# The start of a decoder layer: the first two weight chunks in two halves each, their transfers on two queues, three more warm-up matmuls

## The chip, the cores and the metric

One core of one Trainium2 chip runs the whole kernel. The metric is the time of one execution on the device in microseconds (us). Kernels are compared by the median of several executions; the profile is of one further execution, taken with the hardware profiler.

## The reference

The kernel computes one layer of a hybrid decoder for a sequence of 256 tokens with 1024 features, all in float32, and a last RMS norm:

```
h = rms_norm(x, norm_mix)
z = h @ w_in                      # 1024 -> 3072 columns
a_x, a_y, b_q, b_f, b_i, b_g, c_q, c_k, c_v = split(z)
y = concat(norm(rglru(a_x, a_y)), hgrn2(b_q, b_f, b_i, b_g), norm(attention(c_q, c_k, c_v)))
x = x + y @ w_out
x = x + square(relu(rms_norm(x) @ w_ff1)) @ w_ff2
return rms_norm(x)
```

For this case only the beginning matters: the input projection h @ w_in, and what of the HGRN2 group follows first. That group takes b_f through a sigmoid (forget gate and key) and b_q through a silu (query), and multiplies the two.

## The kernel before, in words

**Precision by splitting.** Each float32 matrix is split into a high part that TensorE (PE) takes in one pass and a low part, the remainder. A product is then three matmuls: high by high, high by low, low by high (`mm3`, L275 to L279). The high part is a copy on ScalarE (ACT, L59), the low part a subtraction on VectorE (DVE, L60), which waits for the copy. For weights this is `split_w`, for the transposed input `x_split` (L130): the gain of the norm goes in there, while the norm's factor 1/rms, one per token, is applied to the results later.

**Tiles.** x stands transposed in xa, 128 features by 256 tokens in each of eight tiles k = 0 to 7, with a few small parameters in front. w_in comes as 12 chunks of 256 columns; a chunk is 128 x 2048 (1 MB), that is its eight k blocks side by side. A quarter of a chunk (256 KB) holds two k blocks and goes with one piece of x (two tiles). A chunk takes 48 matmuls of 256 columns: eight k blocks, two halves, three products each; that is 12 in each of its four slots. Three buffers hold raw chunks; `split_w` issues the load of chunk i + 3 when it has split the last part of chunk i.

**Order.** The order of work is written out by hand. `slots` (L765) is the list of PE's work, in units such as `in_quarter(i, q)`, a quarter of the matmuls of chunk i. `plan` (L769) says which other steps are put ahead of each slot. Each engine works through its own instructions in that order and waits, by semaphores, for what it needs from the others. In `in_quarter` (L291) chunk 0 goes over k outside and both halves of its columns inside, with two accumulators in the PSUM pool `mis`. All other chunks run one half of the columns over all eight k and then the other half, in one bank of the pool `acc`, which has four.

**Transfers.** All are issued by SyncE (SP). At the front it issues, in turn, the four pieces of x and the four quarters of chunk 0 (L100 to L104), then chunk 1 in four quarters, chunk 2 in two halves, and two small tensors (L107, L108). While this goes on, PE runs 9 matmuls on the identity into `warm` (L115), which nobody reads.

**Steps that the text names.** `small_lb` (L247): a few tiny operations on ACT, then on GpSimd (POOL), then on DVE (`omlb`, `lbm`). `x_sq` and `x_sum` (L190, L193): squares of x on ACT, and their sum over the eight tiles on DVE, three additions. `x_ss` (L198): sums over the features on PE (`xss`). `x_rms` (L204): 1/rms on DVE (`xv`) and POOL (`rx`). `x_bc` and `x_rb` (L210, L216): PE spreads rx over all partitions (`xbc`), ACT copies it to `RB`. `hg_f_ev` and `hg_q_ev` (L321, L334): DVE multiplies the results of chunks 0 and 1 by RB. `hg_f_act`, `hg_q_act`, `hg_q_dve` (L325 to L341): sigmoids and silu on ACT, each with a table load, and their product `qk` on DVE. `hg_dqk` (L348): PE matmuls on qk. Chunk 0 is b_f, chunk 1 b_q, chunk 2 b_g.

Of the kernel before, what the change touches and what calls it, by code (L numbers as in the profile page):

```python
# [8 lines left out]
F32 = mybir.dt.float32  # L9
# [3 lines left out]
OP = mybir.AluOpType  # L13
AX = mybir.AxisListType

P = 128
# [16 lines left out]
def trunk_kernel(ctx: ExitStack, tc, x, x_t, w_in, w_out, w_ff1, w_ff2, small, hg_norm, norm_final, out):  # L33
    nc = tc.nc
    V, A, G, T = nc.vector, nc.scalar, nc.gpsimd, nc.tensor
# [3 lines left out]
    raw_p = ctx.enter_context(tc.tile_pool(name="raw", bufs=RAW))  # L39
# [6 lines left out]
    def acc(name):  # L46
        return acc_p.tile([P, 512], F32, name=name, tag="acc")

    def mis(name):
        return mis_p.tile([P, 512], F32, name=name, tag="mis")  # L50

    def wt(name, shape, tag=None, bufs=None, dt=F32):
        return work.tile(shape, dt, name=name, tag=tag or name, bufs=bufs)
# [11 lines left out]
    NI = len(in_order)  # L65
    IG, IX, IY = 2, 3, 4
    NF = 16
    chunks = [w_in[c] for c, _ in in_order] + [w_out[j] for j in range(4)]
# [6 lines left out]
    raw, hi_w, lo_w = {}, {}, {}  # L75

    def load(i, n=1):
        if i < NCH:
            raw[i] = raw_p.tile([P, 2048], F32, name=f"raw{i}", tag="raw")
            for h in range(n):  # L80
                s_ = slice(h * 2048 // n, (h + 1) * 2048 // n)
                nc.sync.dma_start(raw[i][:, s_], chunks[i][:, s_])
# [13 lines left out]
    xT = xa[:, SP_WA:].rearrange("p (k t) -> p k t", k=KT)  # L96
    spw = const.tile([P, SP_N - SP_WA], F32, name="spw")
    hgn = const.tile([P, 64], F32, name="hgn")
    raw[0] = raw_p.tile([P, 2048], F32, name="raw0", tag="raw")
    for h in range(4):  # L100
        s_ = slice(h * 512, (h + 1) * 512)
        x_ = slice(SP_WA + h * 512 if h else 0, SP_WA + (h + 1) * 512)
        nc.sync.dma_start(xa[:, x_], x_t[:, x_])
        nc.sync.dma_start(raw[0][:, s_], chunks[0][:, s_])  # L104
    load(1, 4)
    load(2, 2)
    nc.sync.dma_start(spw, small)  # L107
    nc.sync.dma_start(hgn, bass.AP(tensor=hg_norm.tensor, offset=hg_norm.offset, ap=[[0, P], [1, 64]]))  # L108
# [3 lines left out]
    ident = const.tile([P, P], F32, name="ident")  # L112
    make_identity(nc, ident)
    warm = mis("warm")
    for n in range(9):  # L115
        T.matmul(warm[:, 0:128], ident, ident, start=True, stop=True)

    def rms_scale(ss, n, k, name):
# [38 lines left out]
    for L in LEVELS:  # L157
        n = 64 // L
# [27 lines left out]
    RB = wt("RB", [P, 256])  # L186
# [32 lines left out]
    def zT(i, dst):  # L219
        V.tensor_tensor(dst, z[i][2].rearrange("p (c t) -> p c t", c=2), RBb, op=OP.mult)  # L220
# [52 lines left out]
    z = {}  # L273
# [7 lines left out]
    def in_mm(i, half, k):  # L281
        o = z[i][half]
        s_ = slice(half * 128, (half + 1) * 128)
        wh = hi_w[i].rearrange("p (k c) -> p k c", c=CW)[:, k, :]
        wl = lo_w[i].rearrange("p (k c) -> p k c", c=CW)[:, k, :]
        if in_order[i][1] == CH:
            mm3(o, (wh[:, s_], wl[:, s_]), (hTh[:, k, :], hTl[:, k, :]), k == 0, k == KT - 1)
        else:
            mm3(o, (hTh[:, k, s_], hTl[:, k, s_]), (wh, wl), k == 0, k == KT - 1)

    def in_quarter(i, q):  # L291
        if q == 0:
            if i == 0:
                z[i] = [mis(f"z0{b}")[:, 0:256] for b in range(2)]
            else:
                a = acc(f"z{i}")
                z[i] = [a[:, 0:256], a[:, 256:512], a]
        if i == 0:
            for k in (2 * q, 2 * q + 1):
                for half in range(2):  # L300
                    in_mm(i, half, k)
        else:
            for k in range(4 * (q % 2), 4 * (q % 2) + 4):
                in_mm(i, q // 2, k)
# [8 lines left out]
    qc = wt("qc", [P, 2, 256])  # L313
# [18 lines left out]
            V.tensor_scalar(kB[:, c, :], kB[:, c, :], omlb[:, c:c + 1], None, op0=OP.mult)  # L332

    def hg_q_ev():  # L334
        zT(1, qc)

    def hg_q_act():
        A.activation(flat(qc), flat(qc), AF.Silu)
# [417 lines left out]
    def x1_ss():  # L756
        for t in range(2):
# [4 lines left out]
    r2 = wt("r2", [P, 2])  # L762
    nfb = wt("nfb", [P, D], tag="oc")
    S_ = split_w
    slots = [(in_quarter, i, q) for i in range(NI) for q in range(4)]  # L765
    slots += [(wout_part, k, t, n) for k in range(4) for t, n in tn]
    slots += [(wout_part, k, t, n) for t, n in tn for k in range(4, 8)]
    slots += [(ff1_first, c, kg) for kg in range(2) for c in range(2)]
    plan = {  # L769
        0: [  # L770
            (S_, 0, 0, 4), (x_split, 0), (x_split, 3), (x_split, 1), (S_, 0, 1, 4), (x_split, 5), (x_split, 4),
            (x_split, 2), (x_split, 7), (x_split, 6),
        ],
        1: [(S_, 0, 2, 4)],
        2: [(S_, 0, 3, 4), (S_, 1, 0, 4)],
        3: [(small_lb,), (S_, 1, 1, 4)],
        4: [(S_, 1, 2, 4), (x_sq, 0)],
        5: [(S_, 1, 3, 4), (x_sq, 1)],
        6: [(x_sum,)],
        7: [(x_ss,), (x_rms,), (small_lam,), (S_, 2, 0), (S_, 2, 1)],  # L780
        9: [(x_bc,), (S_, 3, 0), (S_, 3, 1)],
        10: [(x_rb,)],
        11: [(S_, 4, 0)],
        12: [(hg_f_ev,), (hg_q_ev,), (S_, 4, 1), (hg_f_act,)],
        13: [(S_, 5, 0), (hg_q_act,), (hg_q_dve,)],
        14: [(hg_f_dve,)],
# [66 lines left out]
    i = FI + 2  # L853
# [114 lines left out]
```

## Time and profile before

| | |
|---|---|
| median of 3 runs | 323.9 us (323.85, 323.9, 326.06) |
| profiled execution | 325.72 us |
| its span | 324.0 us |
| PE busy | 313.3 us (97%) |
| VectorE busy | 200.5 us (62%) |
| ScalarE busy | 172.3 us (53%) |
| GpSimd busy | 30.1 us (9%) |
| bytes moved by DMA | 54.65 MB, 169 GB/s on average |

The span is the time from the first to the last thing that the profiler records; the rest of the execution's time lies around it. All times in the rows count from the start of the span. A busy share of PE says that instructions were in it, not at which clock they ran. Matmuls overlap, so the distance of their starts is the time that one costs, and their own duration is longer. In the rows, PEld is PE's loading of the stationary operand, and SPq the queue of SyncE, which issues transfers.

### The profile page before, as it was taken

The page shows a single profiled execution, that of the slowest core. Times are in us where ns is not written, and L with a number is a line of the kernel's source. Part 1 is how long each engine was busy: PE and PEld are TensorE (multiplying, and loading weights), DVE is VectorE, ACT ScalarE, POOL GpSimd, SP SyncE. Part 2 cuts the span into 40 slices and gives each one's busy share as a digit, 9 for nine tenths or more (in the row PEclk, how much of TensorE's full clock was granted, in tenths as well). Part 3 has the DMA queues.
Part 4 walks back from the last instruction along what each step waited for, and adds up shares of the span by engine and source line. Part 5 has one row for each costly group of instructions (what it writes and reads, how often), then busy time and mean ns, then how long its engine had stood idle before and what let it go on. Part 6 is the DMA issues. An engine that isn't in the chain of part 4 may idle for free.

```text
span 324.0 us, 5150 instructions
## 1 busy us (share of the span) xinstructions
PE 313.3 (97%) x2090; PEld 286.1 (88%) x2090; DVE 200.5 (62%) x288; ACT 172.3 (53%) x281; POOL 30.1 (9%) x76
## 2 busy tenths in 40 slices
PE   6999999999999999999999999999999999999990
PEld 5899999988899988998898899889889988988980
DVE  1778999997736385498637635743763574376334
ACT  3968796665665372398525633652563365256114
POOL 8428600000002000000000000000000000000002
PEclk9999999999999999999999999999999999999998
DMA  7967353342018327038763365346336524630003
GB/s 195 364 260 284 143 225 131 131 138 121 2 31 358 131 95 296 0 132 324 261 259 141 129 251 224 99 199 259 144 122 254 227 92 202 261 129 3 0 0 129
DMA packets 9960, 54.65 MB, mean 169 GB/s; under 512 B 1232, under 2 KB 1488, under 8 KB 4176
## 3 DMA queue, kind: packets, MB, share of 16 engines
q1 hardware_dynamic: 9936, 54.32, 44.9%
q8 instruction: 16, 0.26, 0.3%
q14 instruction: 8, 0.07, 0.1%
HBM read 53.27 MB, written 1.05 MB: 168 GB/s over the span
## 4 chain that ended last, share of the span: by engine, by line
PE 94%; DMA 2%; issue 1%; ACT 1%; SPq 1%; POOLq 0%; POOL 0%; DVE 0%
PE f L277 9%; PE f L278 9%; PE f L279 9%; PE fo L278 9%; PE fo L277 9%; PE fo L279 9%; PE z L277 7%; PE z L278 7%; PE z L279 7%; PE wo L277 2%; PE wo L278 2%; PE wo L279 2%; DMA xa<-in_x_t_dram 2%; PE lv L372 2%; PE s L593 1%; PE pt L613 1%
## 5 line engine op out<-in xcount | busy, mean ns | idle before, releaser
L60 DVE TENSOR_TENSOR wl<-raw,wh 128x1024 fp32r<-128x1024 f32 (+1 forms) x100 | 112.9, 1179 | 17.2 <-ACT wh L59 15.4
L59 ACT CAST wh<-raw 128x1024 fp32r<-128x1024 f32 (+1 forms) x100 | 95.1, 1009 | 5.2 <-DMA raw<-in_w_in_dram 5.2
L277 PE MATMUL f<-x1h,wh 128*128 128x256 f32 x256 | 72.4, 283 | 0.0
L278 PE MATMUL f<-x1l,wh 128*128 128x256 f32 x256 | 72.4, 283 | 0.0
L279 PE MATMUL f<-x1h,wl 128*128 128x256 f32 x256 | 72.3, 283 | 0.0
L721 ACT ACTIVATE fr<-f 128x512 f32<-128x512 f32 (+1 forms) x17 | 9.7, 572 | 86.9 <-PE f L279 86.9
L723 DVE TENSOR_TENSOR fu<-fr 128x512 f32<-128x512 f32 (+1 forms) x17 | 11.2, 660 | 69.2 <-ACT fr L721 69.2
L278 PE MATMUL fo<-wl,uh 128*128 128x512 f32 x128 | 51.1, 399 | 0.0
L277 PE MATMUL fo<-wh,uh 128*128 128x512 f32 x128 | 50.4, 394 | 0.0
L279 PE MATMUL fo<-wh,ul 128*128 128x512 f32 x128 | 50.2, 392 | 0.0
L277 PEld LDWEIGHTS f<-x1h,wh 128*128 128x128 f32 x256 | 49.0, 191 | 0.7
L278 PEld LDWEIGHTS f<-x1l,wh 128*128 128x128 f32 x256 | 48.9, 191 | 0.6
L279 PEld LDWEIGHTS f<-x1h,wl 128*128 128x128 f32 x256 | 49.0, 191 | 0.0
L277 PE MATMUL z<-hTh,wh 128*128 128x256 f32 x128 | 38.9, 304 | 1.6 <-ACT hTh L131 1.6
L278 PE MATMUL z<-hTl,wh 128*128 128x256 f32 x128 | 37.8, 295 | 0.1
L279 PE MATMUL z<-hTh,wl 128*128 128x256 f32 x128 | 37.2, 291 | 0.0
L279 PEld LDWEIGHTS fo<-wh,ul 128*128 128x128 f32 x128 | 24.0, 188 | 5.7
L277 PEld LDWEIGHTS fo<-wh,uh 128*128 128x128 f32 x128 | 24.1, 188 | 5.5
L278 PEld LDWEIGHTS fo<-wl,uh 128*128 128x128 f32 x128 | 24.0, 188 | 4.9
L277 PEld LDWEIGHTS z<-hTh,wh 128*128 128x128 f32 x128 | 25.6, 200 | 2.6 <-ACT hTh L131 2.2
L278 PEld LDWEIGHTS z<-hTl,wh 128*128 128x128 f32 x128 | 25.6, 200 | 0.8 <-DVE hTl L132 0.7
L279 PEld LDWEIGHTS z<-hTh,wl 128*128 128x128 f32 x128 | 25.6, 200 | 0.0
(204 smaller groups left out, 424.2 us busy)
## 6 DMA issues: line engine op xcount, KB each, us to landing
raw<-in_w_ff_dram SPq DMA_DIRECT2D x32, 1024.0 KB, 4.8
raw<-in_w_in_dram SPq DMA_DIRECT2D x9, 1024.0 KB, 4.8
raw<-in_w_out_dram SPq DMA_DIRECT2D x4, 1024.0 KB, 4.8
raw<-in_w_in_dram SPq DMA_DIRECT2D x8, 256.0 KB, 6.8
raw<-in_w_in_dram SPq DMA_DIRECT2D x2, 512.0 KB, 6.3
xa<-in_x_dram SPq DMA_DIRECT2D x2, 512.0 KB, 7.3
xa<-in_x_t_dram SPq DMA_DIRECT2D x3, 256.0 KB, 6.8
out_dram<-ot SPq DMA_DIRECT2D x3, 256.0 KB, 2.0
```

The lines of the kernel that those rows point to most:

```text
L59: A.copy(hi, src)
L60: V.tensor_tensor(lo, src, hi.bitcast(F32), op=OP.subtract)
L277: T.matmul(o, lh, rh, start=first, stop=False)
L278: T.matmul(o, lh, rl, start=False, stop=False)
L279: T.matmul(o, ll, rh, start=False, stop=last)
L372: T.matmul(ps[:, g * 128:(g + 1) * 128], kB[:, hp, hs], rhs, start=True, stop=True)
L593: T.matmul(ps[:, 128:384], q[rows, c, 128:256], k[rows, c, 0:256], start=True, stop=True)
L613: T.transpose(pt[:, j * 128:(j + 1) * 128], pr_t[h][:, j * 128:(j + 1) * 128], ident)
L721: A.activation(r[:, s_], src, AF.Relu)
L723: V.tensor_tensor(u[:, s_], r[:, s_], r[:, s_], op=OP.mult)
```

## The change

The first two chunks are worked on together: PE takes the first two quarters (k = 0 to 3) of chunk 0, then those of chunk 1, then the last two quarters of chunk 0 and of chunk 1. For this chunk 1 gets two accumulators of its own from the pool `acc`, as chunk 0 has two from `mis`, and `hg_q_ev` reads them in two instructions. The four quarters of chunk 0 are issued by ScalarE; SyncE issues the pieces of x and chunk 1 in the new order. 12 instead of 9 matmuls on the identity run at the start. The plan of slots 0 to 11 is written anew: the x tiles are split in their order, `small_lb` follows the second quarter of chunk 1, `x_sum` stands between the two splits of chunk 2, `x_ss` and `x_rms` move from slot 7 to slot 9, `x_bc` from slot 9 and `x_rb` from slot 10 to slot 11. From slot 12 on the plan is the same.

```diff
-    raw[0] = raw_p.tile([P, 2048], F32, name="raw0", tag="raw")
-    for h in range(4):
-        s_ = slice(h * 512, (h + 1) * 512)
+    for i in range(2):
+        raw[i] = raw_p.tile([P, 2048], F32, name=f"raw{i}", tag="raw")
+
+    def part(eng, i, a, b):
+        eng.dma_start(raw[i][:, a * 512:b * 512], chunks[i][:, a * 512:b * 512])
+
+    def x_part(h):
         x_ = slice(SP_WA + h * 512 if h else 0, SP_WA + (h + 1) * 512)
         nc.sync.dma_start(xa[:, x_], x_t[:, x_])
-        nc.sync.dma_start(raw[0][:, s_], chunks[0][:, s_])
-    load(1, 4)
+
+    x_part(0)
+    part(nc.scalar, 0, 0, 1)
+    x_part(1)
+    part(nc.scalar, 0, 1, 2)
+    part(nc.sync, 1, 0, 1)
+    part(nc.scalar, 0, 2, 3)
+    part(nc.sync, 1, 1, 2)
+    part(nc.scalar, 0, 3, 4)
+    x_part(2)
+    x_part(3)
+    part(nc.sync, 1, 2, 4)
     load(2, 2)
...
-    for n in range(9):
+    for n in range(12):
         T.matmul(warm[:, 0:128], ident, ident, start=True, stop=True)
...
+            elif i == 1:
+                z[i] = [acc(f"z1{b}")[:, 0:256] for b in range(2)]
             else:
                 a = acc(f"z{i}")
                 z[i] = [a[:, 0:256], a[:, 256:512], a]
-        if i == 0:
+        if i < 2:
             for k in (2 * q, 2 * q + 1):
                 for half in range(2):
                     in_mm(i, half, k)
...
     def hg_q_ev():
-        zT(1, qc)
+        for c in range(2):
+            V.tensor_tensor(qc[:, c, :], z[1][c], RB, op=OP.mult)
...
-    slots = [(in_quarter, i, q) for i in range(NI) for q in range(4)]
+    slots = [(in_quarter, i, 2 * h + q) for h in range(2) for i in range(2) for q in range(2)]
+    slots += [(in_quarter, i, q) for i in range(2, NI) for q in range(4)]
...
-        0: [
-            (S_, 0, 0, 4), (x_split, 0), (x_split, 3), (x_split, 1), (S_, 0, 1, 4), (x_split, 5), (x_split, 4),
-            (x_split, 2), (x_split, 7), (x_split, 6),
-        ],
-        1: [(S_, 0, 2, 4)],
-        2: [(S_, 0, 3, 4), (S_, 1, 0, 4)],
-        3: [(small_lb,), (S_, 1, 1, 4)],
-        4: [(S_, 1, 2, 4), (x_sq, 0)],
-        5: [(S_, 1, 3, 4), (x_sq, 1)],
-        6: [(x_sum,)],
-        7: [(x_ss,), (x_rms,), (small_lam,), (S_, 2, 0), (S_, 2, 1)],
-        9: [(x_bc,), (S_, 3, 0), (S_, 3, 1)],
-        10: [(x_rb,)],
-        11: [(S_, 4, 0)],
+        0: [(S_, 0, 0, 4), (x_split, 0), (x_split, 1)],
+        1: [(S_, 0, 1, 4), (x_split, 2), (x_split, 3)],
+        2: [(S_, 1, 0, 4)],
+        3: [(S_, 1, 1, 4), (small_lb,)],
+        4: [(S_, 0, 2, 4), (x_split, 4), (x_split, 5)],
+        5: [(S_, 0, 3, 4), (x_split, 6), (x_split, 7)],
+        6: [(S_, 1, 2, 4), (x_sq, 0)],
+        7: [(S_, 1, 3, 4), (x_sq, 1)],
+        8: [(S_, 2, 0), (x_sum,), (S_, 2, 1)],
+        9: [(x_ss,), (x_rms,), (small_lam,), (S_, 3, 0), (S_, 3, 1)],
+        11: [(x_bc,), (x_rb,), (S_, 4, 0)],
         12: [(hg_f_ev,), (hg_q_ev,), (S_, 4, 1), (hg_f_act,)],
         13: [(S_, 5, 0), (hg_q_act,), (hg_q_dve,)],
```

## Rows read from the trace of the kernel before

**Rows 1.** Page, part 1: engine, busy us, share of the span, instructions.

```profile
PE 313.3 (97%) x2090; PEld 286.1 (88%) x2090; DVE 200.5 (62%) x288; ACT 172.3 (53%) x281; POOL 30.1 (9%) x76
```

**Rows 2.** PE's waits, whole run: us in total, times, longest us.

```profile
PE z L277 <- ACT hTh L131: 1.6, 2, 1.1
```

**Rows 3.** Window of PE on tile z: stretch, us, PE busy (matmuls), clock, DMA, GB/s.

```profile
6.80:14.16 7.36, 6.77 (x26) 1.00 1.01 366
```

**Rows 4.** Timeline of PE: start us, us, what, xcount, [idle before <-releaser].

```profile
1.46 4.21 PE L116 MATMUL warm<-ident 128*128 128x128 f32 x18 [1.46 <-POOL ident masks.py:199]
...
6.82 0.58 PE L277 MATMUL z<-hTh,wh 128*128 128x256 f32 x1 [1.14 <-ACT hTh L131]
...
10.87 0.58 PE L277 MATMUL z<-hTh,wh 128*128 128x256 f32 x1 [0.44 <-ACT hTh L131]
...
21.27 0.56 PE L201 MATMUL xss<-ones,xsq 128*128 128x64 f32 x4
...
23.15 0.28 PE L277 MATMUL z<-wh,hTh 128*128 128x256 f32 x1
...
24.63 0.60 PE L213 MATMUL xbc<-ident,rx 128*128 128x128 f32 x4
...
35.15 0.33 PE L351 MATMUL dqk<-bones,qk 128*128 128x64 f32 x2
```

**Rows 5.** Chain that ended last: start us, us on the chain, what.

```profile
12.22 0.21 PE z L277
...
14.95 0.12 PE z L277
```

**Rows 6.** Timeline of SP's queue, front.

```profile
0.81 0.38 SPq L103 DMA_DIRECT2D xa<-in_x_t_dram  x1
1.24 0.42 SPq L104 DMA_DIRECT2D raw<-in_w_in_dram  x1
...
10.87 0.33 SPq L107 DMA_DIRECT2D spw<-in_small_dram  x1
11.55 0.33 SPq L108 DMA_DIRECT2D hgn<-in_hg_norm_dram  x1
```

**Rows 7.** Timeline of ACT.

```profile
5.74 0.62 ACT L59 CAST wh<-raw 128x512 fp32r<-128x512 f32 x1 [3.65 <-DMA raw<-in_w_in_dram]
...
8.84 0.62 ACT L59 CAST wh<-raw 128x512 fp32r<-128x512 f32 x1 [0.45 <-DMA raw<-in_w_in_dram]
...
13.24 0.20 ACT L236 ACTIVATE sm<-sm 128x2 f32<-128x2 f32 x1
...
14.79 1.05 ACT L191 ACTIVATE xsq<-xa 128x1024 f32<-128x1024 f32 x1
...
17.22 1.98 ACT L59 CAST wh<-raw 128x1024 fp32r<-128x1024 f32 x2
...
25.27 0.37 ACT L217 COPY RB<-xbc 128x256 f32<-128x256 f32 x1 [3.01 <-PE xbc L213]
```

**Rows 8.** Timeline of DVE.

```profile
10.10 2.20 DVE L132 SCALAR_TENSOR_TENSOR hTl<-xa,hTh 128x256 fp32r<-128x256 f32 x5
12.32 1.90 DVE L60 TENSOR_TENSOR wl<-raw,wh 128x512 fp32r<-128x512 f32 x3
15.37 0.17 DVE L253 TENSOR_SCALAR omlb<-lb 128x2 f32<-128x2 f32 x1 [1.15 <-POOL lb L245]
...
17.35 1.23 DVE L194 TENSOR_TENSOR xsq<-xsq 128x1024 f32<-128x1024 f32 x1
...
19.34 0.43 DVE L196 TENSOR_TENSOR xsq<-xsq 128x256 f32<-128x256 f32 x1
...
21.94 5.92 DVE L60 TENSOR_TENSOR wl<-raw,wh 128x1024 fp32r<-128x1024 f32 x5
...
33.06 0.70 DVE L341 TENSOR_TENSOR qk<-qc,kB 128x512 f32<-128x512 f32 x1 [0.72 <-ACT qc L338]
```

## The prediction

> **What bounds the kernel now.** I read the busy shares first: PE is busy 313.3 of 324.0 us [rows 1]. A busy matmul row need not mean full pace, so the next view is PE's waits over the whole run: after the warm-up there are only two, both of the input projection on hTh, 1.6 us in all [rows 2]. From 10.87 us to the tail PE never waits. So whatever changes the time has to act either on the stretch before that, or on the order of later work so strongly that PE begins to wait again.
>
> Then I looked at the pace. In the stretch from 6.82 to 14.16 us the matmuls start 0.21 us apart, later 0.12 us [rows 5]. 256 columns in 0.21 us is the 1.2 GHz level; 0.12 us belongs to the 2.4 GHz level. The granted clock column says 1.00 there all the same [rows 3], so the pace has to be read from the spacing. Before the rise PE had worked without a pause since 10.87 us; ahead of that it had stood 1.14 us before the first projection matmul and 0.44 us before the thirteenth [rows 4]. 26 matmuls lie in that stretch of 7.34 us [rows 3]; at 0.12 us they would take 3.1 us. **4.2 us is therefore the most that the front can give**, 1.3% of the run.
>
> **The change, part by part.** The sum is made against the profiled execution: 325.72 us, of which the span is 324.0 us. That is 1.8 us above the median of 323.9 us.
>
> *More warm-up.* 18 records take 4.21 us [rows 4], 0.234 us each; 24 take 5.6 us and end near 7.07 us instead of 5.67. The first real matmul came at 6.82, so the three extra ones cost at most 0.25 us there and close the pause of 1.14 us.
>
> *Issue from ScalarE.* ACT issues four transfers before its first table load. SP needs 0.42 us for one, with starts 0.43 to 0.47 us apart [rows 6], so ACT has about 2 us of extra work in a stretch in which it waits for the first weights until 5.74 us [rows 7]. I cost this at nothing; if the weights came before about 4 us, it would delay the first cast. SP has four fewer issues ahead of its second chunk and of the small tensors behind it.
>
> *Landing.* Eight pieces of 256 KB (in either version) must land before 48 matmuls can run. Before, SP's last issue of the front, at 11.55 us, marks the landing of the eighth, because SP holds a new transfer back until an older one has landed; at the end pieces come 0.68 us apart (10.87 and 11.55) [rows 6]. Ends for the change: one piece later (+0.7 us), since the two queues interleave; or, had all pieces after the first weights (5.74) come 0.68 us apart, 9.8 us, which is 1.7 us earlier. I take 0.5 us earlier, nearer to no gain, because issues at 0.47 us run far ahead of landings: issuing was not what held the pieces back. The Trainium skill says the same in "DMA: Bandwidth & Descriptors", Issuing engines are not separate DMA queues: a second issuing engine saves only sequencer time, the transfers share the same DMA engines. By that rule the shift is 0 and the result half a microsecond later than by my choice.
>
> *Order of the halves.* The second quarter of chunk 0 no longer waits for x tile 2 behind tiles 5 and 4: ACT casts w01 at 8.84 [rows 7] and the x tiles 2 and 3 follow, so its matmuls start near 10.0 instead of 10.87. At full pace three quarters of 12 x 0.12 = 1.44 us bring PE to about 14.7 us.
>
> *The wait on small_lb.* Here DVE stops. The step now stands ahead of the split of w02. In the old trace the chain from ACT's exp (13.24) to DVE's omlb took until 15.54, 2.30 us, and DVE stood 1.15 us for it [rows 7, 8]; only chunk 1 was behind it. Now w02, w03, four low x tiles and everything after are behind it. With landing as before: w11 at 11.55, its cast 0.62 at most [rows 7], exp at 12.1, DVE free at 14.4. PE needs the low parts of w02 and x tile 4 at 14.7 and gets them at 14.4 + 0.63 + 0.44 = 15.5. Four more quarters then end near 21.2 us. Before, they ended at 23.15 less 0.36 us of xss matmuls: 22.8. **Gain up to here 1.6 us**, and this hardly depends on the clock: at the slow pace PE would reach 14.7 later, but DVE would still be there at 15.5.
>
> *x_sum between the two splits of chunk 2.* From 14.4 DVE has four weight splits (0.63 each, 2.52), four low x tiles (2.20/5 each, 1.76), the first split of chunk 2 (5.92/5 = 1.18), x_sum (17.35 to 19.77, 2.42) and the second split (1.18): 9.06 us, to 23.5 [rows 8]. ACT delivers the cast of chunk 2 late (four casts, four x tiles, two squares of 1.05 and half of 1.98 after 12.7 [rows 7]), about 0.8 us of waiting, so 24.3. PE, at 22.6 with the first quarter of chunk 2, waits for xss and then for this split. That quarter ends near 25.6, the next at 27.0. **More than half of the gain is gone.**
>
> *x_bc two slots later.* xbc moves from slot 9, 24.63 us, to slot 11, about 27.0. RB hangs on it, and on RB a chain on ACT and DVE without a pause: RB copy at 25.27 after 3.01 us of waiting, two casts, table load, two sigmoids, a cast, table load, silu, and qk on DVE, done at 33.76 [rows 7, 8]. From xbc's start that is 9.13 us. PE wants qk for dqk in slot 16, which was 35.15 [rows 4]: the slack was 1.39 us. Two slots fewer between the two are 2 x 1.44 = 2.88 us, so **PE now waits about 1.5 us at dqk**, a wait that did not exist. dqk starts at 27.0 + 9.13 = 36.1, that is 1.0 us later than before with landing unchanged, 0.5 us with my landing. Behind it DVE's next items (kB, qbd) are just in time for slot 17, and from there PE is continuous again, so the half microsecond stays to the end.
>
> *PSUM.* z1 takes two accumulators; z4 then waits for the evacuation of z1 instead of using a free one. That falls in slots 12 and 16, more than 3 us apart; nothing. Two half evacuations in place of one cost a few tenths on DVE behind the table load.
>
> **Sum:** 325.72 + 0.5 = 326.2 in an execution like the profiled one. Now the median. The two short runs (323.85, 323.90) lie 1.8 us below it. Part of that could be an earlier rise of PE's clock in them: the 14 matmuls from 10.87 to 14.16 at 0.12 would save 1.3 us. This part would not carry over, since the changed front is held by DVE at either pace. Then the result is 326.2 - 0.5 = 325.7. If all 1.8 us carry over, 324.4. One trace cannot separate these; I take 324.7, nearer to the second because nothing shows the first.
>
> **The rivals.**
> - *The gain is kept.* If the pieces land a microsecond or more earlier, lb is out of the way before PE gets there, and if ACT makes up time before qk, 1.6 us and a little more reach the end: about 323.0. For: the early pieces land far apart (5.74, 8.84) against 0.68 later. Against: the slack of 1.39 us is a fixed length and two slots exceed it.
> - *The clock.* With the pause before 6.82 closed, the 26 slow matmuls run at 0.12: 26 x 0.09 = 2.3 us; carried through in full, 325.7 - 2.3 = 323.4 or, from the median, as low as 321.6. The Trainium skill, "TensorE: Matmul & The Clock Gate", Why this matters for your kernels, advises continuous work to reach and hold the upper level. The old trace agrees, with 3.3 us of unbroken work ahead of the rise. Against: at that pace PE waits for pieces and DVE instead.
> - *Slower than before.* The interleaving of the two queues delays the eighth piece. From one piece (0.7 us) on, the chain through lb, the second split of chunk 2, xbc and qk passes every tenth on: 1.0 + 0.7 = 1.7, or 327.4 in an execution like the profiled one.
> - *It does nothing.* Clock and landing as before: this is the forecast at +1.0, since the order alone makes it.
>
> **Chances.** Forecast 0.60, gain kept 0.18, clock 0.10, slower 0.12. The forecast's own range is 323.6 to 326.4. For 8 in 10 I reach down to 322.1 for most of the two faster cases and up to 326.7. A difference under 1% (320.7 to 327.1) can't be told from no change: inside it 0.88, faster 0.05, slower 0.07. The ceiling of 4.2 us leaves little for over 1% faster.
>
> **What would show it.** After: matmuls 0.12 us apart well before 14 us; PE waiting near 14.7 for a low part on DVE; DVE idle over 1 us ahead of omlb; PE waiting for wl of chunk 2 near 23 to 24 us; xbc near 27; a new wait of dqk on qk, 1 to 2 us, the largest one of PE. Wrong, if dqk does not wait, if the eighth piece lands before 10.5, or if PE stays at 0.21 us past 14 us.

## The result and the profile after

The changed kernel takes 326.17 us (median of 9 runs, 325.96 to 327.62); before took 323.9 us in the same set (9 runs, 323.65 to 326.15). The ratio is 1.0063, 95% interval 1.0034 to 1.0092: 2.0 us slower, 1.1 to 3.0; the medians differ by 2.3 us. That is 0.6%, inside the 1% in which the prediction had put 0.88 of its chances, and inside its range; its single number, 324.7, was 1.5 us too low. The profiled execution takes 326.17 us with a span of 324.5, against 325.72 and 324.0 before: 0.45 us more, where the sum had said 0.5.

One fact is needed to read these numbers. The times of one kernel fall into groups: before, 6 of 9 runs lie from 323.65 to 324.18 and 3 near 326; after, 6 lie from 325.96 to 326.18 and 3 near 327.6. The profile of before is of its upper group, that of after of its lower. Experiments 4, 5 and 9 are about what makes the groups.

First the busy time of the page, then PE's waits over the whole run (us in total, times, longest), both of the changed kernel.

```profile
PE 312.4 (96%) x2096; PEld 285.1 (88%) x2096; DVE 200.4 (62%) x289; ACT 172.2 (53%) x281; POOL 26.1 (8%) x76
```

```profile
PE dqk L368 <- DVE qk L358: 1.5, 1, 1.5
PE warm L130 <- POOL ident masks.py:199: 1.5, 1, 1.5
PE z L292 <- DVE hTl L146: 0.9, 2, 0.5
PE xss L215 <- DVE xsq L210: 0.3, 1, 0.3
PE z L292 <- DVE wl L60: 0.2, 1, 0.2
```

Before there were two waits behind the warm-up, both ahead of 11 us [rows 2]. Now there are four kinds, and the largest, dqk on qk, did not exist. Where they lie shows in the timeline of PE, changed kernel.

```profile
1.47 5.49 PE L130 MATMUL warm<-ident 128*128 128x128 f32 x24 [1.47 <-POOL ident masks.py:199]
...
6.62 0.58 PE L291 MATMUL z<-hTh,wh 128*128 128x256 f32 x1
...
7.57 0.29 PE L293 MATMUL z<-hTh,wl 128*128 128x256 f32 x1
7.70 0.28 PE L291 MATMUL z<-hTh,wh 128*128 128x256 f32 x1
...
14.72 0.39 PE L292 MATMUL z<-hTl,wh 128*128 128x256 f32 x1 [0.54 <-DVE hTl L146]
...
20.45 0.28 PE L291 MATMUL z<-wh,hTh 128*128 128x256 f32 x1
...
22.32 0.63 PE L215 MATMUL xss<-ones,xsq 128*128 128x64 f32 x4 [0.28 <-DVE xsq L210]
...
23.37 0.38 PE L292 MATMUL z<-wl,hTh 128*128 128x256 f32 x1 [0.24 <-DVE wl L60]
...
26.22 0.60 PE L227 MATMUL xbc<-ident,rx 128*128 128x128 f32 x4
...
35.49 1.08 PE L368 MATMUL dqk<-bones,qk 128*128 128x64 f32 x8 [1.48 <-DVE qk L358]
```

Against [rows 4]: the projection starts at 6.62 without the pause of 1.14 us, and from 7.57 us the matmuls are 0.12 us apart; in the execution of [rows 5] that came only after 14 us. Chunks 0 and 1 are done at 20.45 instead of 22.8 (23.15 less the xss matmuls): **2.3 us gained**. Then it is given back. From 20.45 to xbc at 26.22 us PE has three quarters (3 x 1.44 us) and xss (0.36 us) to do and takes 5.77 us, so 1.1 us go at the two stops at xss and at the second split of chunk 2. (The profile marks them with 0.28 and 0.24 us of idle time only; the ends of matmuls are modelled, so I count by starts.) The rest, and 0.34 us more, goes at dqk, where PE stands 1.48 us. xbc is 1.6 us later than before, dqk 0.34 us.

A part of the 2.3 us is not the new order. The execution of before that is profiled has the late rise of the pace; against one with the old order and an early rise (experiment 4) the gain up to the same point is 1.0 us.

The other side of these waits, in the timelines of ACT and then DVE, changed kernel.

```profile
0.80 2.08 ACTq L103 DMA_DIRECT2D raw<-in_w_in_dram  x4
2.91 1.28 ACT L59 ACT_TABLE_LOAD   x1 [2.91 <-issue]
...
10.93 0.62 ACT L59 CAST wh<-raw 128x512 fp32r<-128x512 f32 x1 [0.73 <-DMA raw<-in_w_in_dram]
...
17.56 1.98 ACT L59 CAST wh<-raw 128x1024 fp32r<-128x1024 f32 x2
...
26.86 0.37 ACT L231 COPY RB<-xbc 128x256 f32<-128x256 f32 x1 [4.19 <-PE xbc L227]
```

```profile
13.43 0.17 DVE L267 TENSOR_SCALAR omlb<-lb 128x2 f32<-128x2 f32 x1 [1.16 <-POOL lb L259]
...
18.63 1.23 DVE L60 TENSOR_TENSOR wl<-raw,wh 128x1024 fp32r<-128x1024 f32 x1 [0.97 <-ACT wh L59]
19.77 1.22 DVE L208 TENSOR_TENSOR xsq<-xsq 128x1024 f32<-128x1024 f32 x1
...
22.09 1.22 DVE L60 TENSOR_TENSOR wl<-raw,wh 128x1024 fp32r<-128x1024 f32 x1
...
34.64 0.70 DVE L358 TENSOR_TENSOR qk<-qc,kB 128x512 f32<-128x512 f32 x1 [0.71 <-ACT qc L355]
```

The second quarter of chunk 1, w11, is there at 10.93 us, 0.6 earlier than the eighth piece before, whose place the sum gave it, and no earlier than the seventh (10.87) [rows 6]. The stop at omlb is 1.16 us long. From xbc to the end of qk it is 35.34 - 26.22 = 9.12 us, as before (9.13). Behind the omlb stop there is a second one on DVE, 0.97 us for ACT's cast of chunk 2; it becomes important in the third experiment.

### The profile page after: what moved, and what is told of

Its sections match the earlier page's. It is cut to its first block, busy times and chain, and to the rows that moved or that the text cites. A ratio compares the mean times of both kernels' runs of the same rounds, so it can differ in the third digit from the quotient of the medians.

```text
span 324.5 us, 5161 instructions
## 1 busy us (share of the span) xinstructions
PE 312.4 (96%) x2096; PEld 285.1 (88%) x2096; DVE 200.4 (62%) x289; ACT 172.2 (53%) x281; POOL 26.1 (8%) x76
## 4 chain that ended last, share of the span: by engine, by line
PE 87%; ACT 5%; DMA 3%; DVE 2%; issue 1%; SPq 0%; POOLq 0%; POOL 0%
PE f L291 9%; PE f L292 9%; PE f L293 9%; PE fo L292 9%; PE fo L291 9%; PE fo L293 9%; PE z L291 5%; PE z L292 5%; PE z L293 5%; DMA raw<-in_w_in_dram 3%; PE wo L291 2%; PE wo L292 2%; PE wo L293 2%; PE lv L389 2%; ACT wh L59 2%
## 5 line engine op out<-in xcount | busy, mean ns | idle before, releaser
L291 PE MATMUL z<-hTh,wh 128*128 128x256 f32 x128 | 37.7, 294 | 0.0
L292 PE MATMUL z<-hTl,wh 128*128 128x256 f32 x128 | 36.5, 285 | 1.0 <-DVE hTl L146 0.9
L293 PE MATMUL z<-hTh,wl 128*128 128x256 f32 x128 | 36.1, 282 | 0.0
L292 PEld LDWEIGHTS z<-hTl,wh 128*128 128x128 f32 x128 | 24.5, 191 | 1.8 <-DVE hTl L146 1.7
L291 PEld LDWEIGHTS z<-hTh,wh 128*128 128x128 f32 x128 | 24.5, 192 | 0.5 <-issue 0.3
L293 PEld LDWEIGHTS z<-hTh,wl 128*128 128x128 f32 x128 | 24.5, 191 | 0.0
```

The source lines that it names most:

```text
L291: T.matmul(o, lh, rh, start=first, stop=False)
L292: T.matmul(o, lh, rl, start=False, stop=False)
L293: T.matmul(o, ll, rh, start=False, stop=last)
```

## The experiments

The theory: the front's gain is real, and xbc two slots later takes it away, since the chain from xbc to qk has a fixed length. Rivals: the stop at omlb, or the first split of chunk 2, holds everything; or the clock decides. Kernels of one set ran on one chip, each 12 times, beside 29 to 35 runs of before. Those medians (325.27, 325.22 and 324.39 us) depend on how many of before's runs fall into its lower group (15 of 35, 14 of 35, 15 of 29), so I compare groups as well as medians. In the second set the groups run into each other; the 14 are those up to 324.6 us. The changed kernel was not run again in these sets: its 326.17 us is from the set of the result. Three variants that leave dqk where it was (3, 5 and 9) came out at 325.94 to 326.06 us, one in each set, so the sets differ little.

**1. Before, with xbc two slots later and nothing else.**

```
-        9: [(x_bc,), (S_, 3, 0), (S_, 3, 1)],
-        10: [(x_rb,)],
-        11: [(S_, 4, 0)],
+        9: [(S_, 3, 0), (S_, 3, 1)],
+        11: [(x_bc,), (x_rb,), (S_, 4, 0)],
```

> The kernel before with x_bc and x_rb in slot 11 and nothing else changed. Slack theory: qk comes 9.1 us after xbc and dqk wanted it with 1.39 us to spare; two slots (2.88 us) use that up, so dqk waits about 1.5 us on qk and the run is 1.4 to 1.5 us slower than before. Rival (the split of chunk 2 and the lb wait cost the time, not the place of x_bc): no wait at dqk, time as before.

Measured 327.46 us against 325.27, ratio 1.0069 (1.0036 to 1.0102): 2.2 us, 1.2 to 3.3. PE's waits and the tile xbc (durations in ns, first and last start):

```profile
PE z L277 <- ACT hTh L131: 1.6, 2, 0.8
PE dqk L351 <- DVE qk L341: 1.5, 1, 1.5
...
L213 PE MATMUL xbc<-ident,rx x4: 270/274/275, 28.6 to 28.9; 128*128 128x128 f32 x4
```

The wait appears in a kernel whose front is untouched, with the length that the slack gave (2.88 - 1.39 = 1.49). The place of x_bc alone makes it. The time rose by more than the wait, though its interval holds 1.5 us. In the profiled execution (328.49 us) most of the excess is at the front: the spacing stays 0.21 us until 16.66 us, later than in [rows 5], and xss comes at 22.32 us where it was 21.27. Behind dqk the pace is full (stretch, us, PE busy, granted clock, DMA, GB/s):

```profile
39.00:40.00 1.00, 1.00 (x11) 1.00 0.00 0
```

What made the other eleven runs longer or shorter is not shown.

**2. The changed kernel, with xbc one slot earlier.**

```
-        11: [(x_bc,), (x_rb,), (S_, 4, 0)],
+        10: [(x_bc,), (x_rb,)],
+        11: [(S_, 4, 0)],
```

> The changed kernel with x_bc and x_rb in slot 10 instead of 11. Slack theory: rx is there near 25.0 us, slot 10 begins at 24.8, so xbc starts at 25.0 to 25.1 instead of 26.2, RB and qk come 1.1 to 1.2 us earlier, the wait of 1.5 us at dqk shrinks to under 0.5 and the run is 1.1 us faster than the changed kernel. Rival (DVE alone is late whatever the place of x_bc): under 0.3 us.

Measured 324.97 us, all twelve from 324.78 to 325.07: 1.2 us below the changed kernel. The tiles xbc and dqk:

```profile
L227 PE MATMUL xbc<-ident,rx x4: 275/275/376, 24.9 to 25.4; 128*128 128x128 f32 x4
...
L368 PE MATMUL dqk<-bones,qk x8: 275/275/295, 34.3 to 35.1; 128*128 128x64 f32 x8
```

dqk starts 1.2 us earlier, the wait at dqk is gone from the list of PE's waits, and so is the upper group.

**3. The stop at omlb taken away.**

```
         g(lb, lbr, lbr, OP.subtract)
+
+    def small_lb_dve():
         V.tensor_scalar(omlb, lb, -1.0, 1.0, op0=OP.mult, op1=OP.add)
...
-        8: [(S_, 2, 0), (x_sum,), (S_, 2, 1)],
+        8: [(S_, 2, 0), (x_sum,), (S_, 2, 1), (small_lb_dve,)],
```

> The changed kernel with omlb and lbm on DVE moved from slot 3 to the end of slot 8; the steps on ACT and POOL stay. By the prediction's step DVE is free 1.2 us earlier and all behind it with it: xbc and dqk 0.5 to 1.1 us earlier. By the rival, read from the chain of the changed kernel, ACT sets the pace (from the landing of w11 at 10.9 us to the cast of chunk 2 at 18.6 it never pauses, and DVE waits 0.97 us for that cast): the wait of PE at 14.7 us goes, but the first split of chunk 2 still starts at 18.6 and the time stays within 0.2 us.

Measured 326.06 us, against 326.17 of the changed kernel: no difference that can be told. PE's waits, and DVE's first split of chunk 2:

```profile
PE dqk L370 <- DVE qk L360: 1.5, 1, 1.5
...
PE xss L215 <- DVE xsq L210: 0.7, 1, 0.7
```

```profile
18.39 1.23 DVE L60 TENSOR_TENSOR wl<-raw,wh 128x1024 fp32r<-128x1024 f32 x1 [1.21 <-ACT wh L59]
```

PE's stop near 14.7 is gone and its stop at xss grew from 0.3 to 0.7. DVE has lost the 1.16 us stop and waits longer for ACT instead (1.21 for 0.97). The first split starts 0.24 us earlier, no more than the landing of w11 was earlier in this execution (its cast at 10.68). So my step on small_lb described a stop that was there and cost nothing at the end: ACT, busy from the landing of w11 to the cast of chunk 2, was the chain.

**4. Before, with 12 warm-up matmuls** (`range(9)` to `range(12)`).

> The kernel before with 12 warm-up matmuls. Clock theory: the times of before fall into two groups, near 323.8 and near 326, because PE's clock rises early in some executions and near 14 us in others; with the pause before 6.8 us filled it rises early always, so all runs lie near 323.8 and the profile shows 0.12 us spacing well before 14 us. Rival (the groups come from something else): two groups as before, or all runs later by up to 0.2 us.

Measured 324.01 us, ratio 0.9977 (0.9953 to 1.0000). 9 of 12 runs from 323.46 to 324.39, 3 near 325.5; before in the same set 15 of 35 in the lower group, a difference that by itself could be chance. In the profile, an execution of the lower group with a span of 322.7 us, the spacing is 0.12 us from 7.19 us on. PE then stops longer than before for x tile 2, since it arrives earlier (timeline of PE, with the start of chunk 2, xbc and dqk):

```profile
10.64 0.38 PE L277 MATMUL z<-hTh,wh 128*128 128x256 f32 x1 [1.61 <-ACT hTh L131]
...
21.80 0.28 PE L277 MATMUL z<-wh,hTh 128*128 128x256 f32 x1
...
23.29 0.60 PE L213 MATMUL xbc<-ident,rx 128*128 128x128 f32 x4
...
33.80 1.00 PE L351 MATMUL dqk<-bones,qk 128*128 128x64 f32 x8
```

Against the execution of [rows 4] chunk 2, xbc and dqk all come about 1.35 us earlier, and the time is 1.33 us shorter; 0.24 us of that is earlier landing (SP's last issue of the front at 11.31 us, before at 11.55), the rest the pace. Against this one the changed kernel had chunks 0 and 1 done 1.0 us earlier (20.45 for 21.80 less xss), xbc 2.9 us later and dqk 1.7 us later, nearly all of the 1.8 us between their times. In the profiled executions, then, the late rise goes with the upper group. Other runs point the same way: in the third set 10 of before's 14 upper runs have a mean granted clock of 0.981 or 0.982, and none of its 15 lower ones is under 0.991. The warm-up does not empty the upper group; no profile shows what is behind those three runs.

**5. The changed kernel with 9 warm-up matmuls** (`range(12)` to `range(9)`).

> The changed kernel with 9 warm-up matmuls instead of 12. Clock theory: PE pauses near 5.7 us again and the spacing of 0.12 us begins later, in some executions only near 14 us; from then on PE reaches the waits on DVE later by up to 1.4 us, so more runs lie in the upper group (near 327.5 us) than with 12. In executions that rise early the time is that of the changed kernel, 326.1. Rival (the warm-up does nothing here, because DVE holds PE at either pace): same times and the same single main group.

Measured 325.95 us: 9 runs from 325.78 to 326.10, 3 from 327.35 to 327.57, the same picture as with 12. The warm-up does nothing for the median here. But the profile is of the upper group (327.57 us), and its front is not at fault: 0.12 us spacing from 7.53, dqk at 35.34, earlier than in the changed kernel's own profile. The loss comes behind dqk. PE in stretches of 1 us (stretch, us, PE busy, granted clock, DMA, GB/s), and its timeline there:

```profile
34.00:35.00 1.00, 0.00 (x0) 1.00 1.04 442
35.00:36.00 1.00, 0.66 (x6) 1.00 0.91 385
36.00:37.00 1.00, 1.00 (x8) 0.67 0.09 16
37.00:38.00 1.00, 1.00 (x7) 0.50 0.00 0
38.00:39.00 1.00, 1.00 (x6) 0.50 0.03 8
39.00:40.00 1.00, 1.00 (x8) 0.62 0.00 0
40.00:41.00 1.00, 1.00 (x11) 1.00 0.60 82
```

```profile
35.34 1.08 PE L368 MATMUL dqk<-bones,qk 128*128 128x64 f32 x8 [1.48 <-DVE qk L358]
...
36.49 0.41 PE L292 MATMUL z<-hTl,wh 128*128 128x256 f32 x1
36.70 0.41 PE L293 MATMUL z<-hTh,wl 128*128 128x256 f32 x1
```

After the stop of 1.48 us the granted clock is 0.50, the 1.2 GHz level, and matmuls are 0.21 us apart; from 40 us on it is 1.00 again, with 11 matmuls in 1 us. **The wait at dqk costs twice:** its own length always, and in a part of the executions 1.4 to 1.6 us more through the clock, the distance of the two groups in the changed kernel and here.

**6. The changed kernel with all transfers on SP** (`part(nc.scalar, ...)` to `part(nc.sync, ...)`).

> The changed kernel with all transfers issued by SP, in the same order. The chain from the landing of w11 (10.9 us) to dqk has no pause, so the time moves as that landing does. By the prediction's choice the second queue brought 0.5 us, so +0.5 us without it. By the rule that queues share the transfer engines, nothing: w11 is the seventh piece, and the seventh landed at 10.87 us in the kernel before, so within 0.2 us of the changed kernel.

Measured 326.87 us, from 325.88 to 328.28, spread wider than any other. In its profile (328.28 us, with the clock's fall behind dqk) w11 and dqk come at

```profile
11.49 0.62 ACT L59 CAST wh<-raw 128x512 fp32r<-128x512 f32 x1 [0.28 <-DMA raw<-in_w_in_dram]
```

```profile
36.04 1.13 PE L368 MATMUL dqk<-bones,qk 128*128 128x64 f32 x8 [1.47 <-DVE qk L358]
```

0.56 and 0.55 us later than with two queues: the landing passes through to dqk undiminished, and the second queue is worth about what I chose, 0.5 us, in this pair of executions. In the medians it is 0.7 us, with groups that overlap, so the size is not firm. In the seven profiled executions of the changed kernel and its variants with two queues, w11's cast starts between 10.58 and 10.93 us; with one queue there is this one. How far one queue scatters shows in the old order of transfers, where SP's last issue of the front, which waits for the eighth piece, lies at 11.55 us before, at 11.50 and 11.31 in experiments 1 and 4, and at 10.38 in experiment 10. The Trainium skill, "DMA: Bandwidth & Descriptors", Issuing engines are not separate DMA queues, grants a second issuing engine only sequencer time. Here, with the same pieces issued in the same order, w11 landed earlier; whether by more than the time that ACT's issues save SP is not shown.

**7. The sum first, and xbc in slot 10.**

`small_lb_dve` is that of experiment 3.

```
...
+        8: [(x_sum,), (x_ss,), (S_, 2, 0), (x_rms,), (small_lb_dve,), (small_lam,), (S_, 2, 1)],
+        9: [(S_, 3, 0), (S_, 3, 1)],
+        10: [(x_bc,), (x_rb,)],
+        11: [(S_, 4, 0)],
```

> The changed kernel with x_sum and x_ss ahead of the first split of chunk 2, x_rms between its two splits, x_bc and x_rb in slot 10, omlb and lbm on DVE in slot 8. Order theory: xbc near 24.2 us instead of 26.2, dqk near 33.5 instead of 35.5, 2.0 us faster than the changed kernel, with PE waiting about 0.6 us for the first split of chunk 2 and under 0.4 at dqk. Rival (the front gives no more than xbc in slot 10 did): 1.1 us faster, as with xbc in slot 10 alone.

Measured 323.86 us, 323.66 to 324.15, ratio to before 0.9956 (0.9933 to 0.9978); 2.3 us below the changed kernel. PE:

```profile
23.80 0.61 PE L227 MATMUL xbc<-ident,rx 128*128 128x128 f32 x4
...
33.07 1.08 PE L370 MATMUL dqk<-bones,qk 128*128 128x64 f32 x8
...
35.47 1.07 PE L391 MATMUL lv<-qbd,kB 128*128 128x128 f32 x8
```

What is won ahead of xbc arrives at the end once xbc is early enough: 2.4 us less at dqk, 2.3 in the time. Against before nearly all of the gain is that no run falls into an upper group: before's lower group lies from 323.4 to 324.6 us in this set, with a median of 324.0.

**8. Two steps more:** the first addition of x_sum in halves (`x_half`, put ahead of what is left of x_sum), and the cast of chunk 5 behind silu and qk.

```
...
+    def x_half(h):
+        V.tensor_tensor(xsq[:, 4 * h:4 * h + 2, :], xsq[:, 4 * h:4 * h + 2, :], xsq[:, 4 * h + 2:4 * h + 4, :], op=OP.add)
...
-        13: [(S_, 5, 0), (hg_q_act,), (hg_q_dve,)],
+        13: [(hg_q_act,), (hg_q_dve,), (S_, 5, 0)],
```

> As the run with x_sum first, and two steps more: the first addition of x_sum is split, one half done while ACT still squares the other four tiles, and the cast of chunk 5 stands behind silu and qk. DVE reaches the first split of chunk 2 0.6 us earlier and the chain from xbc to qk is 1.0 us shorter, so no wait at dqk is left: dqk near 32.7 us, 2.8 us faster than the changed kernel, near 323.3 us and 0.5 us below the lower group of the kernel before. Rival (a wait moves on behind dqk, because chunk 5 is cast later): no faster than the run with x_sum first.

Measured 323.64 us, 323.37 to 323.85, ratio 0.9958 (0.9938 to 0.9978). dqk comes at

```profile
32.70 1.00 PE L372 MATMUL dqk<-bones,qk 128*128 128x64 f32 x8
...
35.27 1.15 PE L393 MATMUL lv<-qbd,kB 128*128 128x128 f32 x8
```

as expected, but the time is 0.2 us below that of the sum first and not the 0.6 that 323.3 us would have been, and the split in halves moved the first split of chunk 2 by 0.17 us (19.50 for 19.67) and not by 0.6. With the sum first the list of PE's waits has none at dqk and its starts show 0.2 us there, so a chain shorter by 1.0 us had little to take away. Of the 0.37 us at dqk 0.20 are left at lv, PE's next step: a wait moved on behind dqk, as the rival said.

**9. The stop at dqk filled with work.**

```
         ps_h["d"] = mis("dqk")
+        for n in range(6):
+            T.matmul(ps_h["d"][:, 0:128], ident, ident, start=True, stop=True)
```

> The changed kernel with six matmuls on the identity (12 records) in front of dqk, written into dqk's own accumulator and then overwritten. PE's wait of 1.5 us for qk is filled with work, qk comes no earlier. Clock theory: in a part of the executions the stop of 1.5 us lets the clock fall to 1.2 GHz for some 4 us, which costs 1.4 us more and makes the upper group near 327.5; without the stop this group is gone and all runs lie near 326.1 (at most 0.2 later, if the fill outlasts the wait). Rival (the upper group comes from the front of the run): the upper group stays, about a quarter of the runs.

Measured 325.94 us, all twelve from 325.75 to 326.05. PE's timeline and, in a window of its own, its clock behind dqk:

```profile
33.70 1.50 PE L368 MATMUL dqk<-ident 128*128 128x128 f32 x12
35.25 1.10 PE L370 MATMUL dqk<-bones,qk 128*128 128x64 f32 x8
```

```profile
36.00:40.00 4.00, 4.00 (x37) 1.00 0.01 2
```

From xbc (26.07 us) to dqk it is 9.18 us, in the changed kernel 9.27, so the lower group stays where it was; the upper one, 3 of 9, 3 of 12 and 3 of 12 runs in the changed kernel and experiments 3 and 5, is gone. (The kernels of 1 and 6 stop there too; their runs spread too widely to count groups.) Twelve runs alone could be chance, but the kernels of experiments 2, 7 and 8, which do not stop long at dqk, have no upper group either: none in 48 runs, against 9 in 33. The stop made it.

**10. Before, x tiles in order and 12 warm-up matmuls,** without the halves.

```
-            (S_, 0, 0, 4), (x_split, 0), (x_split, 3), (x_split, 1), (S_, 0, 1, 4), (x_split, 5), (x_split, 4),
-            (x_split, 2), (x_split, 7), (x_split, 6),
-        ],
-        1: [(S_, 0, 2, 4)],
-        2: [(S_, 0, 3, 4), (S_, 1, 0, 4)],
+            (S_, 0, 0, 4), (x_split, 0), (x_split, 1), (S_, 0, 1, 4), (x_split, 2), (x_split, 3),
+        ],
+        1: [(S_, 0, 2, 4), (x_split, 4), (x_split, 5)],
+        2: [(S_, 0, 3, 4), (x_split, 6), (x_split, 7), (S_, 1, 0, 4)],
```

> The kernel before with its x tiles split in their order (0, 1, then 2, 3 behind w01, 4, 5 behind w02, 6, 7 behind w03) and 12 warm-up matmuls; chunks one after the other, one queue, x_bc in slot 9. If the gain of the front is in the order of the x tiles and the warm-up: the second quarter starts near 10 us instead of 10.9, PE never stops longer than 1 us, xbc comes near 22.8 us, dqk never waits, and all runs lie near 323.2 us. Rival (the two chunks in halves are what gains, since ACT needs fewer x tiles early): 323.8 us, as the lower group of before.

**11. The same with chunk 0 issued from ACT** (`nc.sync` to `nc.scalar` in the line of `raw[0]`). Its result and that of 10 follow together.

> As the run before this with chunk 0 issued from ACT's queue. The run with one queue in the changed kernel came out 0.5 us later at dqk than with two; if that holds here, 0.3 to 0.5 us faster than with one queue, near 322.8 us. Rival (the pieces of chunk 0 and x only trade places): the same time as with one queue.

Measured 324.02 us (323.47 to 324.29; ratio 0.9977, 0.9956 to 0.9997) with one queue and 323.61 us (323.19 to 324.06; ratio 0.9962, 0.9943 to 0.9982) with two. Neither has an upper group. In their profiles dqk starts at 32.87 and 32.96 us, without a wait. Both medians miss what was expected (323.2 and 322.8 us) by 0.8 us: with one queue it is the rival's number, 323.8 us, the lower group of before, though the profiled execution (323.47 us, the fastest of the twelve) has the earlier front. The median with two queues is 0.4 us lower, as expected, but the two profiled executions do not show it: SP's last issue of the front is at 10.71 us with two queues and at 10.38 with one.

So two versions beat both kernels, and about equally: the halves with the sum in halves (experiment 8, 323.64 us) and the old order of chunks with x in order, 12 warm-up matmuls and two queues (323.61 us). Against before's lower group (medians 324.0 and 323.9 us in the two sets) either gains 0.3 to 0.4 us; the rest of their lead is that no run falls into an upper group. The halves are not needed for it.

## Why the prediction was right, point by point

*What bounds the kernel.* Right. Of the 0.45 us between the two profiled executions 0.34 are there at dqk, and PE's waits name the place. The ceiling of 4.2 us leaves out that the first projection matmul itself can come earlier than 6.82 us, as it does here (6.62); nothing hangs on that.

*Warm-up.* Right: 24 records end near 7 us, the pause is closed, 0.12 us spacing starts at 7.57. Right too that this is worth nothing in the changed kernel, because PE then waits for others: with 9 warm-up matmuls the median is the same (experiment 5).

*Issue and landing.* Right in size: 0.6 us earlier in the profile than the sum without a gain had it, 0.56 us by experiment 6, where I took 0.5. That the second queue is the reason rests on that one pair of executions and on medians that are 0.4 and 0.7 us apart.

*The halves.* The gain up to the end of chunk 1 was 2.3 us against 1.6 with landing unchanged, 2.1 with the landing I took. That it "hardly depends on the clock" holds for the changed kernel alone. Before's side depends on it: against an execution with the old order and an early rise the gain is 1.0 us (experiment 4).

*The wait on small_lb.* The stop was there with its length (1.16 us) and its effect on PE at 14.7 us, but the step's conclusion failed: that everything behind it is late because of it. Experiment 3 took it away and the time did not move. I had counted ACT's casts, tiles and squares as a wait of 0.8 us on top; they were the longer of two parallel chains, and an addition should have been a maximum. In the sum this cost little: with my landing the second split of chunk 2 was to end at 23.8 us, and it ended at 23.3.

*x_sum and x_bc.* Right: 5.77 us from the end of chunk 1 to xbc (5.8 in the forecast, 21.2 to 27.0), xbc at 26.2 (26.5 with my landing), a wait of 1.48 us at dqk (1.5), dqk 0.34 us later (0.5). Experiments 1 and 2 show the mechanism from both sides.

*From the profiled execution to the median.* **This is the step that was off.** The sum gave 326.2 for an execution like the profiled one, and 325.7 if before's short runs owed 1.3 us of their lead to an early rise of the clock; I took 324.7, since nothing showed that. Experiment 4 shows it in a pair of executions, 1.35 us at dqk, and in experiments 10 and 11, where the x tiles are in order as well, no run is left in the upper group. Where PE waits for qk anyhow, the early rise gives nothing, so the changed kernel had no share in that lead, nor in the 0.5 us that the 325.7 still left it, and its median came out at the profiled time.

That the sum met the profile to 0.05 us is partly luck as well: the execution of before was one of the upper group and that of after one of the lower. An execution of after from its upper group (327.55 us) would have stood 1.8 us above.

*Not foreseen.* That the new stop at dqk would bring the clock down in a part of the executions. It moved a quarter to a third of the runs by 1.4 to 1.6 us and left the median alone.

*The rivals.* "The gain is kept" and "the clock" were wrong for this kernel: the pieces did land early and the spacing did improve, and both were lost once the slack of 1.39 us was used up. "Slower through late landing" did not occur. "It does nothing" would have had the same place of the loss without the earlier landing.

## What to carry to other kernels

Before a step is moved in a static order, measure the slack of the chain that hangs on it, from its start to the instruction that wants the end of it: 1.39 us against 2.88 us of moved slots decided this case, and both numbers stood in the old trace. When two engines feed the same point, take the later of the two chains, not their sum. And take the sum against the group of runs that the profiled execution belongs to before comparing with a median.

## What the runs showed of the hardware

A stop of PE of 1.48 us in the middle of unbroken work was followed in some executions by a granted clock of 0.50 and a spacing of 0.21 us, and cost 1.4 to 1.6 us beyond its own length; in others it was not. Of the five profiled executions with that stop two show the fall (experiments 5 and 6) and three do not (the changed kernel, experiments 1 and 3). With twelve records of needless matmuls in the stop no run of twelve was in the upper group. At the start of a run the granted clock reads 1.00 while the spacing is 0.21 us [rows 3, 5], so there only the spacing tells. With the same transfers issued by one queue in the same order, the eighth piece of 256 KB landed between 10.38 and 11.55 us in four executions.
